# Expert weights from one-hot matrices: one multiplication for three parts, and second-key one-hots kept in DRAM

## The chip, the cores and the metric

The kernel runs on one core of a Trainium2 chip. The metric is the device time of one execution in microseconds (us). Engines are named as in the profile: PE multiplies matrices, PEld is its weight load, DVE, ACT and POOL are the vector, scalar and GpSimd engines, SP is the engine whose queue issues the loads of weights.

## The reference

One layer of a decoder trunk on 256 tokens with model width 2048. The first half (a convolution, a dilated attention, two gates) is not touched. The second half retrieves experts:

```python
s = jnp.einsum('bshpe,hpne->bshpn', qp, sub_keys)       # 8 heads, 2 keys of 128
v1, i1 = lax.top_k(s[..., 0, :], 16)
v2, i2 = lax.top_k(s[..., 1, :], 16)
cand = (v1[..., :, None] + v2[..., None, :]).reshape(B, S, 8, 256)
top, ci = lax.top_k(cand, 16)
e1 = jnp.take_along_axis(i1, ci // 16, axis=-1)
e2 = jnp.take_along_axis(i2, ci % 16, axis=-1)
idx = e1 * 128 + e2                                      # 8 x 16 experts of a token
g = jax.nn.softmax(top, axis=-1)
...
u = jnp.take(w_up, ic, axis=0)
a = jax.nn.gelu(jnp.einsum('td,tkd->tk', xc, u))
return jnp.einsum('tk,tkd->td', gc * a, jnp.take(w_down, ic, axis=0))
```

Everything is float32, and there are 128 x 128 = 16384 experts.

## The kernel before

The kernel does not gather. It computes the activation of every expert for every token (`up_unit`), multiplies it by a gate that is zero for the experts that a token did not choose, and multiplies the result by all of `w_down` (`down_unit`). Experts are counted by the first key e1 (128 rows of 128 experts), and rows go in four quarters q of EQ = 32. Two buffers, `CB[0]` and `CB[1]`, hold one quarter each.

A float32 weight is split in two float32r parts: ACT copies it into `hi` (`split_a`, L84), and DVE or POOL subtracts to give `lo` (`split_b`, L88). A product is then three matmuls: hi by hi, hi by lo, lo by hi. Of an up half (1024 of a row's 2048 columns) DVE first transposes the 32 x 32 blocks (`wt`, L1250).

The gate is made by `gate_c(p)`. For p = 0 it serves quarters 0 and 1, for p = 1 quarters 2 and 3. It works on blocks of NT = 8 tokens, 32 blocks in all. The partitions are the 128 (head, choice) pairs of a token. `build(b)` makes on DVE three things in bfloat16: `oh2`, the one-hots of the second key (128 values x 8 tokens); `oh1`, the one-hots of the first key (64 values x 8 tokens, those of the two quarters); and `ohg`, oh1 times each of three bfloat16 parts of the gate weight, which together give its float32 value (`gp`, made in `topk`). Tokens are interleaved in pairs, so that the innermost dimension has two tokens. `product(b)` is 24 matmuls on PE (L1347), 8 tokens by 3 parts, with oh2 of a token as weights (128 columns) and ohg as the moving operand (64 columns), into `gps` in PSUM. `apply(b)` multiplies one half of gps into `CB[0]` on DVE (L1354) and copies the other half into `CB[1]` on ACT (L1359). A step of the generator emits apply(b-2), build(b) and product(b-1) in this order.

The stream `st` puts everything in order by hand. For each half s it emits the ACT copy of half s+3, the subtraction of half s+2, then what is due (the step of the gate), then the matmuls of half s. In the two stretches of this document one step of the gate goes with each half:

- The first stretch (p = 0) runs beside up units of quarter 1, whose `lo` is all made by POOL (`busy`).
- The second stretch (p = 1) runs beside the down units of quarter 1 with d = 1, whose `lo` is all made by DVE. Eight of its 32 rows (`whole and n == 1`) are not split: PE multiplies them in float32 (`mm_whole`, L1458), straight from the loaded weight and from `CB`, and neither ACT nor DVE touches them.

For a split row, ACT also copies the row of C into `cch` (L1413) and DVE subtracts it into `ccl` (L1418). Buffers: four raw tiles of 1 MB, four of `hi`, three of `lo`, two of `wt`, `oh2` and `ohg`, one of `oh1`. In the profile oh1 and oh2 are both named `oh`: L1331 makes oh2, L1334 oh1, L1338 ohg. The tile `CB[..]` is named `C`.

Of the kernel before, what the change touches and what calls it, by code (L numbers as in the profile page):

```python
# [10 lines left out]
BF = mybir.dt.bfloat16  # L11
# [3 lines left out]
OP = mybir.AluOpType  # L15
# [3 lines left out]
P = 128  # L19
T = 256  # L20
# [13 lines left out]
EQ = 32  # L34
# [32 lines left out]
def layer_kernel(ctx, tc, x, c, norm1_g, norm2_g, w_ada, b_ada, w_in, conv_dw, conv_db, conv_ln_g,  # L67
                 conv_ln_b, w_conv_out, b_conv_out, q_norm_g, k_norm_g, w_attn_o, w_out, peer_w_q,
                 peer_sub_keys, peer_w_up, peer_w_down, out):
    nc = tc.nc  # L70
# [6 lines left out]
    main = ctx.enter_context(tc.tile_pool(name="main", bufs=1))  # L77
    dram = ctx.enter_context(tc.tile_pool(name="dram", bufs=1, space=bass.MemoryType.DRAM))
    x1_dram = dram.tile([P, 2, D], F32, name="x1_dram")


    def split_a(h, src):
# [157 lines left out]
    T2 = {}  # L240
# [818 lines left out]
    def open_p2():  # L1059
        pool = p2.enter_context(tc.tile_pool(name="p2", bufs=1))  # L1060
        T2["pool"] = pool
        CB[:] = [pool.tile([P, EQ * T], F32, name=f"C{i}") for i in range(2)]
        T2["keys"], T2["keysT"] = CB[0][:, 0:2048], CB[0][:, 2048:4096]
        nc.gpsimd.dma_start(T2["keys"].rearrange("p (a e) -> p a e", a=16),
                            dap(peer_sub_keys, 0, [[P, P], [P * P, 16], [1, P]]))
        T2["scr"] = CB[1]
        it = pool.tile([P, P, 2], BF, name="iota_rep")
        nc.gpsimd.iota(it, pattern=[[1, P], [0, 2]], base=0, channel_multiplier=0, allow_small_or_imprecise_dtypes=True)
        T2["iota"] = it
        T2["e1T"] = pool.tile([P, T], BF, name="e1T")  # L1070
        T2["e2T"] = pool.tile([P, T], BF, name="e2T")
        T2["gp"] = pool.tile([P, 3, T], BF, name="gp")

    def keys_t():
        for a0 in range(0, 16, 4):
# [81 lines left out]
    def topk():  # L1157
# [14 lines left out]
        for t in range(2):  # L1172
            vals, idx = tk["vals", t], tk["idx", t]
            nc.vector.tensor_copy(idb, idx)
            cand = scr[:, 4096:6144]
            v4 = vals.rearrange("p (h q) a -> p h q a", q=2)
            c4 = cand.rearrange("p (h a b) -> p h a b", h=H8, a=TOPK)
            for hs in halves:
                nc.vector.tensor_tensor(c4[:, hs], v4[:, hs, 0, :, None].to_broadcast([P, H8 // 2, TOPK, TOPK]),
                                        v4[:, hs, 1, None, :].to_broadcast([P, H8 // 2, TOPK, TOPK]), op=OP.add)  # L1180
                yield 1.2, 0
            for h in range(0, H8, 2):
                yield from top16([(top[:, b], ci[:, b], cand[:, b * 256:(b + 1) * 256]) for b in (h, h + 1)], 0.42)

            nc.vector.tensor_copy(den[:, 0], top[:, :, 0])
            nc.vector.tensor_tensor(top, top, den[:, 0, :, None].to_broadcast([P, H8, TOPK]), op=OP.subtract)
            nc.scalar.activation(top, top, AF.Exp)

            nc.vector.tensor_scalar(ca, ci, 4, None, op0=OP.logical_shift_right)
            nc.vector.tensor_copy(cab[:, 0], ca)  # L1190
            nc.vector.tensor_scalar(ca, ci, 15, None, op0=OP.bitwise_and)
            nc.vector.tensor_copy(cab[:, 1], ca)
            nc.vector.tensor_reduce(den[:, 1], top, axis=AX, op=OP.add)
            nc.vector.reciprocal(den[:, 1], den[:, 1])
            nc.vector.tensor_tensor(top, top, den[:, 1, :, None].to_broadcast([P, H8, TOPK]), op=OP.mult)
            yield 1.5, 0
            eq = scr[:, 6144:7168].bitcast(BF).rearrange("p (h a k) -> p h a k", h=H8, a=TOPK)
            pr = scr[:, 7168:8192].bitcast(BF).rearrange("p (h a k) -> p h a k", h=H8, a=TOPK)
            i4 = idb.rearrange("p (h q) a -> p h q a", q=2)
            shape = [P, H8 // 2, TOPK, TOPK]  # L1200
            for q in range(2):
                for hs in halves:
                    nc.vector.tensor_tensor(eq[:, hs], cab[:, q, hs, None, :].to_broadcast(shape),
                                            iota16[:, None].to_broadcast(shape), op=OP.is_equal)
                    yield 0.7, 0
                    nc.vector.tensor_tensor(pr[:, hs], eq[:, hs], i4[:, hs, q, :, None].to_broadcast(shape), op=OP.mult)
                    yield 1.2, 0
                    nc.vector.tensor_reduce(ee[:, q, hs], pr[:, hs].rearrange("p h a k -> p h k a"), axis=AX, op=OP.add)
                    yield 1.2, 0
            ts = slice(t * P, (t + 1) * P)  # L1210
            pt = T2["ps"].tile([P, 3, P], F32, name="eT", tag="m", bufs=2)
            yield 0.0, 4
            for q in range(2):
                nc.tensor.transpose(pt[:, q, :], ee[:, q].rearrange("p h k -> p (h k)"), ident)
            nc.tensor.transpose(pt[:, 2, :], top.rearrange("p h k -> p (h k)"), ident)
            nc.scalar.copy(T2["e1T"][:, ts], pt[:, 0, :])
            nc.scalar.copy(T2["e2T"][:, ts], pt[:, 1, :])

            gp = T2["gp"]
            nc.scalar.copy(gp[:, 0, ts], pt[:, 2, :])  # L1220
            nc.vector.tensor_tensor(rest, pt[:, 2, :], gp[:, 0, ts], op=OP.subtract)
            nc.vector.tensor_copy(gp[:, 1, ts], rest)
            nc.vector.tensor_tensor(rest, rest, gp[:, 1, ts], op=OP.subtract)
            nc.vector.tensor_copy(gp[:, 2, ts], rest)
            yield 1.0, 0

    topk_gen = topk()
# [49 lines left out]
    NT = 8  # L1277
    late = []

    def c_row(q, r, n=1):  # L1280
        if q < 3:
            return CB[q % 2][:, r * T:(r + n) * T]
        return CB[1].rearrange("p (b e t) -> p e b t", e=EQ, t=NT)[:, r:r + n]
# [37 lines left out]
    def gate_c(p):  # L1321
        nb = T // NT
        state = {}

        def build(b):

            pairs = lambda v: v.rearrange("p (b t) -> p b t", t=2)
            ts = slice(b * NT, (b + 1) * NT)
            nb2, ne = NT // 2, 2 * EQ
            o2 = T2["pool"].tile([P, nb2, P, 2], BF, name="oh2", tag="oh2", bufs=2)  # L1330
            nc.vector.tensor_tensor(o2, T2["iota"][:, None].to_broadcast([P, nb2, P, 2]),  # L1331
                                    pairs(T2["e2T"][:, ts])[:, :, None].to_broadcast([P, nb2, P, 2]), op=OP.is_equal)
            o1 = T2["pool"].tile([P, nb2, ne, 2], BF, name="oh1", tag="oh1", bufs=1)
            nc.vector.tensor_tensor(o1, T2["iota"][:, None, p * ne:(p + 1) * ne].to_broadcast([P, nb2, ne, 2]),  # L1334
                                    pairs(T2["e1T"][:, ts])[:, :, None].to_broadcast([P, nb2, ne, 2]), op=OP.is_equal)
            og = T2["pool"].tile([P, 3, nb2, ne, 2], BF, name="ohg", tag="ohg", bufs=2)
            for i in range(3):
                nc.vector.tensor_tensor(og[:, i], o1, pairs(T2["gp"][:, i, ts])[:, :, None].to_broadcast([P, nb2, ne, 2]),  # L1338
                                        op=OP.mult)
            state["o", b] = o2, og  # L1340

        def product(b):
            o2, og = state.pop(("o", b))
            ps = T2["ps"].tile([P, NT, 2 * EQ], F32, name="gps", tag="m", bufs=2)
            for t in range(NT):
                for i in range(3):
                    nc.tensor.matmul(ps[:, t, :], lhsT=o2[:, t // 2, :, t % 2], rhs=og[:, i, t // 2, :, t % 2],  # L1347
                                     start=i == 0, stop=i == 2)
            state["p", b] = ps.rearrange("p t e -> p e t")

# [10 lines left out]
        for b in range(nb + 2):  # L1361
            if 0 <= b - 2 < nb:
                apply(b - 2)
            if b < nb:
                build(b)
            if 0 <= b - 1 < nb:
                product(b - 1)
            yield

    gates = [gate_c(p) for p in range(2)]  # L1370
# [13 lines left out]
            return v, c_row(q, rr)  # L1384
        return v.rearrange("p (b t) -> p b t", t=NT), c_row(q, rr)[:, 0]

    def down_unit(q, d, r, whole=False):


        u = Unit(None, [])  # L1390
        e1 = q * EQ + r
# [7 lines left out]
        for n in range(2):  # L1399
# [52 lines left out]
                    for c in range(2):  # L1452
                        products(h, t, c, (1,), False, last)

            def mm_whole(h, rr=rr, n=n):
                for t in range(2):
                    for c in range(2):
                        nc.tensor.matmul(Y["ps"][t][c], lhsT=c_row(q, rr)[:, t * P:(t + 1) * P],  # L1458
                                         rhs=u.raw[:, n * 1024 + c * 512:n * 1024 + (c + 1) * 512], start=False, stop=rr == EQ - 1)

            h.a, h.b, h.mm = a, b, mm
            h.early_b = d == 1
            if whole and n == 1:
                h.a, h.b, h.mm, h.rel = None, None, mm_whole, "m"
            if rr == EQ - 1 and not (q == 3 and d == 1):
                h.after = [lambda: [y_done(q, d, Y["ps"], t, c) for t in range(2) for c in range(2)]]
            u.halves.append(h)
# [61 lines left out]
    for q in range(4):  # L1529
# [8 lines left out]
            add_units([downs[i] if kind else ups[i]], 0.25)  # L1538
        assert q < 1 or not ada_list
        m1 = len(st.halves)  # L1540
        downs = [down_unit(q, 1, r, q == 1 and r % 4 == 2) for r in range(0, EQ, 2)]
        if q == 1:
            for u in downs:
                for h in u.halves:
# [71 lines left out]
```

## Time and profile before

| what | value |
|---|---|
| median of 3 runs | 2517.66 us (2516.47 to 2523.12) |
| profiled execution: its own time | 2518.21 us |
| its span, first to last instruction | 2516.4 us |
| PE busy | 2426.6 us (96%) |
| DVE busy | 1854.2 us (74%) |
| ACT busy | 1120.8 us (45%) |
| POOL busy | 530.3 us (21%) |
| DMA | 518.73 MB, mean 206 GB/s |

The profile counts an instruction as busy from its start to its end, also while it waits for something inside. Spans on POOL are rough. The first stretch lies between 1162.8 and 1310 us of the span, the second between 1849 and 1972 us.

### The profile page before, as it was taken

To read this page: it belongs to the slowest core of one execution; us is meant where nothing else is said; L and a number is where in the kernel's file an instruction comes from. 1 tells how busy PE (TensorE), PEld (TensorE's weight loads), DVE (VectorE), ACT (ScalarE), POOL (GpSimd) and SP (SyncE) were. 2 spreads that over 40 slices of the span, in tenths; PEclk is the share of its full clock that TensorE was granted. 3 is DMA by queue.
4 is the path that set the end of the run, shared out by engine and by line. 5 is a ranking of instruction groups with operands and counts; after the bars stand their busy time and mean duration, and the time that the engine had idled before them with its cause. 6 is when DMAs were issued, how large, how long until landed. Compare 5 with 4: busy or idle time off the path is not lost.

```text
span 2516.4 us, 39750 instructions
## 1 busy us (share of the span) xinstructions
PE 2426.6 (96%) x15728; PEld 2056.6 (82%) x15728; DVE 1854.2 (74%) x2642; ACT 1120.8 (45%) x1477; POOL 530.3 (21%) x262
## 2 busy tenths in 40 slices
PE   7999889999999899988999999999999999999998
PEld 4667677777766799988889988999987899988877
DVE  2655679886454569897998787877799777667776
ACT  5333345444334444443335555555443344445454
POOL 1000000000000007786552234332000111124023
PEclk9999999999999999999999999999999999999999
DMA  9887346777899978777557866899844777766563
GB/s 329 297 301 251 117 136 210 257 251 267 279 298 294 204 159 178 158 167 152 110 124 220 234 218 194 222 226 238 204 156 135 185 181 185 188 186 214 194 209 117
DMA packets 261178, 518.73 MB, mean 206 GB/s; under 512 B 16400, under 2 KB 57568, under 8 KB 260352
## 3 DMA queue, kind: packets, MB, share of 16 engines
q1 hardware_dynamic: 258912, 507.61, 70.4%
q0 software_dynamic: 2048, 8.58, 1.0%
q8 instruction: 123, 2.02, 0.4%
q14 instruction: 63, 0.52, 0.1%
q10 hardware_dynamic: 32, 0.01, 0.0%
HBM read 511.94 MB, written 4.19 MB: 205 GB/s over the span
## 4 chain that ended last, share of the span: by engine, by line
PE 71%; DVE 10%; POOL 3%; issue 2%; DMA 1%; ACT 1%; SPq 0%; DVEq 0%; POOLq 0%; ACTq 0%
PE aps L1267 6%; PE aps L1265 6%; PE aps L1266 6%; PE y L1435 6%; PE y L1436 6%; PE y L1438 5%; PE z L429 5%; PE z L431 4%; PE z L430 4%; PE z L1436 3%; PE z L1438 3%; PE z L1435 3%; POOL lo L88 3%; DVE wt L1250 2%; PE ada L330 2%
## 5 line engine op out<-in xcount | busy, mean ns | idle before, releaser
L88 DVE TENSOR_TENSOR lo<-raw,hi 128x1024 fp32r<-128x1024 f32 x456 | 561.8, 1237 | 376.3 <-issue 112.6
L84 ACT CAST hi<-raw 128x1024 fp32r<-128x1024 f32 x504 | 526.6, 1051 | 520.6 <-PE zv L559 103.1
L1267 PE MATMUL aps<-h2hi,lo 128*128 128x256 f32 x2048 | 582.0, 284 | 8.6 <-POOL lo L88 8.5
L1265 PE MATMUL aps<-h2hi,hi 128*128 128x256 f32 x2048 | 584.3, 285 | 0.4 <-ACT hi L84 0.4
L1266 PE MATMUL aps<-h2lo,hi 128*128 128x256 f32 x2048 | 580.7, 284 | 0.0
L84 ACT CAST hi<-wt 128x1024 fp32r<-128x1024 f32 x256 | 269.3, 1052 | 470.7 <-DVE wt L1250 427.6
L88 POOL TENSOR_TENSOR lo<-wt,hi 128x1024 fp32r<-128x1024 f32 x116 | 292.7, 2529 | 611.1 <-PE aps L1267 497.1
L1267 PEld LDWEIGHTS aps<-h2hi,lo 128*128 128x128 f32 x2048 | 394.0, 192 | 11.2 <-POOL lo L88 11.2
L1265 PEld LDWEIGHTS aps<-h2hi,hi 128*128 128x128 f32 x2048 | 394.1, 192 | 2.6 <-ACT hi L84 0.6
L1266 PEld LDWEIGHTS aps<-h2lo,hi 128*128 128x128 f32 x2048 | 394.3, 193 | 2.0 <-issue 0.2
L1250 DVE STREAM_TRANSPOSE wt<-raw 128x1024 f32<-128x1024 f32 x256 | 315.8, 1237 | 28.2 <-POOL lo L88 23.7
L1418 DVE TENSOR_TENSOR ccl<-C,cch 128x256 fp32r<-128x256 f32 x248 | 198.9, 803 | 96.7 <-PE z L1438 57.6
L1435 PE MATMUL y<-hi,cch 128*128 128x512 f32 x608 | 241.1, 397 | 0.0
L1436 PE MATMUL y<-lo,cch 128*128 128x512 f32 x608 | 237.3, 390 | 0.0
L88 DVE TENSOR_TENSOR lo<-wt,hi 128x1024 fp32r<-128x1024 f32 x140 | 171.8, 1229 | 27.3 <-PE aps L1267 14.0
L1438 PE MATMUL y<-hi,ccl 128*128 128x512 f32 x608 | 187.6, 390 | 0.0
L88 POOL TENSOR_TENSOR lo<-raw,hi 128x1024 fp32r<-128x1024 f32 x48 | 117.0, 2436 | 245.9 <-PE z L1436 123.6
L347 POOL TENSOR_TENSOR acc<-acc,raw 128x512 f32<-128x512 f32 x60 | 101.4, 1689 | 261.0 <-ACT raw L346 240.3
L1413 ACT CAST cch<-C 128x256 fp32r<-128x256 f32 x248 | 99.8, 403 | 123.6 <-PE z L1436 101.9
L1436 PE MATMUL z<-lo,cch 128*128 128x512 f32 x384 | 149.5, 389 | 2.2 <-DVE lo L88 2.2
L1435 PE MATMUL z<-hi,cch 128*128 128x512 f32 x384 | 149.5, 389 | 1.0 <-ACT cch L1413 1.0
L1438 PEld LDWEIGHTS y<-hi,ccl 128*128 128x128 f32 x608 | 114.2, 188 | 24.4
(295 smaller groups left out, 3965.7 us busy)
## 6 DMA issues: line engine op xcount, KB each, us to landing
raw<-in_peer_w_up_dram SPq DMA_DIRECT2D x512, 256.0 KB, 6.0
raw<-in_peer_w_down_dram SPq DMA_DIRECT2D x128, 1024.0 KB, 5.1
raw<-in_w_ada_dram SPq DMA_DIRECT2D x86, 1024.0 KB, 7.1
raw<-in_w_in_dram SPq DMA_DIRECT2D x73, 1024.0 KB, 5.3
raw<-in_w_out_dram SPq DMA_DIRECT2D x64, 256.0 KB, 5.2
raw<-in_peer_w_q_dram SPq DMA_DIRECT2D x64, 256.0 KB, 7.1
raw<-in_w_in_dram SPq DMA_DIRECT2D x22, 512.0 KB, 8.9
raw<-in_w_ada_dram SPq DMA_DIRECT2D x20, 512.0 KB, 5.2
```

The costliest lines, as they stand in the source:

```text
L84: nc.scalar.copy(h.hi, src)
L88: eng.tensor_tensor(h.lo, src, h.hi.bitcast(F32), op=OP.subtract)
L347: nc.gpsimd.tensor_tensor(acc, acc, src, op=OP.add)
L429: nc.tensor.matmul(z, lhsT=ah, rhs=hi[:, kk], start=first, stop=False)
L1250: nc.vector.transpose(wt.rearrange("p j g a -> p g j a"), u.raw.rearrange("p (g j a) -> p g j a", g=4, a=32)[:, :, n * 8:(n + 1) * 8, :])
L1265: nc.tensor.matmul(z, lhsT=hi[:, jj], rhs=qh["hi"][:, j, :], start=j == 0, stop=False)
L1266: nc.tensor.matmul(z, lhsT=hi[:, jj], rhs=qh["lo"][:, j, :], start=False, stop=False)
L1267: nc.tensor.matmul(z, lhsT=lo[:, jj], rhs=qh["hi"][:, j, :], start=False, stop=j == NK - 1)
L1418: nc.vector.tensor_tensor(cl, row, ch, op=OP.subtract)
L1435: nc.tensor.matmul(z, lhsT=ch, rhs=hi, start=first, stop=False)
L1436: nc.tensor.matmul(z, lhsT=ch, rhs=lo, start=False, stop=False)
L1438: nc.tensor.matmul(z, lhsT=cl, rhs=hi, start=False, stop=last)
```

## The change

The three multiplications of oh1 by the parts of the weight become one, with the three parts side by side in `ohg` and in `gp`. The moving operand of a matmul of `product` then steps by 6 elements (12 bytes) in place of 2 (4 bytes). In the first stretch each oh2 is also written to DRAM (256 KB, issued from ACT's queue); in the second stretch it is not computed but read back (256 KB per block, issued from ACT's queue one step ahead, behind product(b-1)). The second stretch has no float32 rows any more: `mm_whole` is gone, and all 32 rows are split.

```diff
+    o2_dram = [dram.tile([P, 1024], BF, name=f"o2_dram{b}") for b in range(T // 8)]
...
-        T2["gp"] = pool.tile([P, 3, T], BF, name="gp")
+        T2["gp"] = pool.tile([P, T // 2, 3, 2], BF, name="gp")
...
-            gp = T2["gp"]
-            nc.scalar.copy(gp[:, 0, ts], pt[:, 2, :])
-            nc.vector.tensor_tensor(rest, pt[:, 2, :], gp[:, 0, ts], op=OP.subtract)
...
+            gp = T2["gp"][:, t * P // 2:(t + 1) * P // 2]
+            pair = lambda v: v.rearrange("p (b t) -> p b t", t=2)
+            nc.scalar.copy(gp[:, :, 0], pair(pt[:, 2, :]))
+            nc.vector.tensor_tensor(pair(rest), pair(pt[:, 2, :]), gp[:, :, 0], op=OP.subtract)
...
+        def fetch(b):
+            o2 = T2["pool"].tile([P, NT // 2, P, 2], BF, name="oh2", tag="oh2", bufs=2)
+            state["o2", b] = o2
+            if p == 1:
+
+                nc.scalar.dma_start(o2.rearrange("p b e t -> p (b e t)"), o2_dram[b])
+
         def build(b):
...
-            o2 = T2["pool"].tile([P, nb2, P, 2], BF, name="oh2", tag="oh2", bufs=2)
-            nc.vector.tensor_tensor(o2, T2["iota"][:, None].to_broadcast([P, nb2, P, 2]),
-                                    pairs(T2["e2T"][:, ts])[:, :, None].to_broadcast([P, nb2, P, 2]), op=OP.is_equal)
+            if p == 0:
+                fetch(b)
+            o2 = state.pop(("o2", b))
+            if p == 0:
+                nc.vector.tensor_tensor(o2, T2["iota"][:, None].to_broadcast([P, nb2, P, 2]),
+                                        pairs(T2["e2T"][:, ts])[:, :, None].to_broadcast([P, nb2, P, 2]), op=OP.is_equal)
+                nc.scalar.dma_start(o2_dram[b], o2.rearrange("p b e t -> p (b e t)"))
...
-            og = T2["pool"].tile([P, 3, nb2, ne, 2], BF, name="ohg", tag="ohg", bufs=2)
-            for i in range(3):
-                nc.vector.tensor_tensor(og[:, i], o1, pairs(T2["gp"][:, i, ts])[:, :, None].to_broadcast([P, nb2, ne, 2]),
-                                        op=OP.mult)
+
+            og = T2["pool"].tile([P, nb2, ne, 3, 2], BF, name="ohg", tag="ohg", bufs=2)
+            shape = [P, nb2, ne, 3, 2]
+            nc.vector.tensor_tensor(og, o1[:, :, :, None].to_broadcast(shape),
+                                    T2["gp"][:, b * nb2:(b + 1) * nb2, None].to_broadcast(shape), op=OP.mult)
...
-                    nc.tensor.matmul(ps[:, t, :], lhsT=o2[:, t // 2, :, t % 2], rhs=og[:, i, t // 2, :, t % 2],
+                    nc.tensor.matmul(ps[:, t, :], lhsT=o2[:, t // 2, :, t % 2], rhs=og[:, t // 2, :, i, t % 2],
...
+            if p == 1 and b == 0:
+                fetch(0)
             if b < nb:
                 build(b)
             if 0 <= b - 1 < nb:
                 product(b - 1)
+            if p == 1 and b + 1 < nb:
+                fetch(b + 1)
...
-            if whole and n == 1:
-                h.a, h.b, h.mm, h.rel = None, None, mm_whole, "m"
...
-        downs = [down_unit(q, 1, r, q == 1 and r % 4 == 2) for r in range(0, EQ, 2)]
+        downs = [down_unit(q, 1, r) for r in range(0, EQ, 2)]
```

## Rows read from the trace of the kernel before

**Rows 1.** Busy time of each engine in three windows, the first stretch in two.

```profile
core 0: us, PE busy (x) PEld busy (x) DVE busy (x) ACT busy (x) POOL busy (x), PEclk, DMA share, GB/s
1173.80:1213.70 39.90, 31.86 (x382) 30.47 (x381) 39.69 (x49) 11.53 (x18) 20.04 (x8) 0.96 0.47 101
1213.70:1308.00 94.30, 88.48 (x1061) 83.38 (x1060) 93.52 (x155) 31.95 (x50) 56.55 (x22) 1.00 0.52 120
1850.00:1968.00 118.00, 117.48 (x1117) 86.53 (x1117) 114.22 (x241) 44.22 (x78) 0.00 (x0) 1.00 0.48 143
```

**Rows 2.** Timeline of DVE, first stretch: start and length in us.

```profile
1173.79 3.30 DVE L1338 TENSOR_TENSOR ohg<-oh,gp 128x512 bf16<-128x512 bf16 x3
...
1202.30 3.24 DVE L1338 TENSOR_TENSOR ohg<-oh,gp 128x512 bf16<-128x512 bf16 x3
...
1213.73 1.09 DVE L1338 TENSOR_TENSOR ohg<-oh,gp 128x512 bf16<-128x512 bf16 x3
...
1222.30 1.10 DVE L1338 TENSOR_TENSOR ohg<-oh,gp 128x512 bf16<-128x512 bf16 x3
1223.31 1.24 DVE L1250 STREAM_TRANSPOSE wt<-raw 128x1024 f32<-128x1024 f32 x1
1224.47 0.39 DVE L1354 TENSOR_TENSOR C<-gps,C 128x256 f32<-128x256 f32 x1
1224.78 1.42 DVE L1331 TENSOR_TENSOR oh<-iota_rep,e2T 128x1024 bf16<-128x1024 bf16 x1
1226.13 0.41 DVE L1334 TENSOR_TENSOR oh<-iota_rep,e1T 128x512 bf16<-128x512 bf16 x1
...
1307.95 1.10 DVE L1338 TENSOR_TENSOR ohg<-oh,gp 128x512 bf16<-128x512 bf16 x3
```

**Rows 3.** Timeline of POOL, first stretch, with idle time before and its releaser.

```profile
1202.66 2.60 POOL L88 TENSOR_TENSOR lo<-wt,hi 128x1024 fp32r<-128x1024 f32 x1 [1.28 <-PE aps L1267]
...
1223.09 2.57 POOL L88 TENSOR_TENSOR lo<-wt,hi 128x1024 fp32r<-128x1024 f32 x1 [1.70 <-PE aps L1267]
```

**Rows 4.** Timeline of PE, first stretch: one product and the next matmul.

```profile
1218.50 1.49 PE L1347 MATMUL gps<-ohg,oh 128*128 128x64 bf16 x24
...
1219.83 0.36 PE L1265 MATMUL aps<-h2hi,hi 128*128 128x256 f32 x1
```

**Rows 5.** Groups by form, 1770 to 1985 us: busy us, mean ns.

```profile
L88 DVE TENSOR_TENSOR lo<-raw,hi 128x1024 fp32r<-128x1024 f32 x34 | 41.5, 1222 | 13.9 <-issue 7.5 <-PE aps L1267 6.4
...
L1338 DVE TENSOR_TENSOR ohg<-oh,gp 128x512 bf16<-128x512 bf16 x96 | 35.1, 421 | 1.1
...
L1331 DVE TENSOR_TENSOR oh<-iota_rep,e2T 128x1024 bf16<-128x1024 bf16 x32 | 21.8, 681 | 0.0
```

**Rows 6.** Chain of waits, second stretch: start, length, what.

```profile
1877.73 3.51 PE y L1458 x8
...
1884.81 0.74 PE gps L1347 x24
...
1885.86 0.23 PE y L1436
...
1888.38 0.74 PE gps L1347 x24
```

**Rows 7.** Timeline of DVE, second stretch: two neighbouring steps.

```profile
1885.06 1.22 DVE L88 TENSOR_TENSOR lo<-raw,hi 128x1024 fp32r<-128x1024 f32 x1
...
1888.93 1.22 DVE L88 TENSOR_TENSOR lo<-raw,hi 128x1024 fp32r<-128x1024 f32 x1
```

**Rows 8.** Timeline of ACT: an issue at the start, then the second stretch.

```profile
0.74 0.42 ACTq L258 DMA_DIRECT2D stage<-in_c_dram  x1
...
1890.91 0.37 ACT L1359 COPY C<-gps 128x256 f32<-128x256 f32 x1 [1.44 <-DVE C L1354]
```

**Rows 9.** DMA issues by line: KB each, median us from issue to landing.

```profile
raw<-in_peer_w_down_dram SPq DMA_DIRECT2D x128, 1024.0 KB, 5.1
...
out_dram<-fin SPq DMA_DIRECT2D x8, 256.0 KB, 2.4
```

More of the change, by code (lines that the diff above doesn't have):

```diff
@@ L1217, in topk @@
             nc.scalar.copy(T2["e2T"][:, ts], pt[:, 1, :])
-            gp = T2["gp"]
-            nc.scalar.copy(gp[:, 0, ts], pt[:, 2, :])
-            nc.vector.tensor_tensor(rest, pt[:, 2, :], gp[:, 0, ts], op=OP.subtract)
-            nc.vector.tensor_copy(gp[:, 1, ts], rest)
-            nc.vector.tensor_tensor(rest, rest, gp[:, 1, ts], op=OP.subtract)
-            nc.vector.tensor_copy(gp[:, 2, ts], rest)
+            gp = T2["gp"][:, t * P // 2:(t + 1) * P // 2]
+            pair = lambda v: v.rearrange("p (b t) -> p b t", t=2)
+            nc.scalar.copy(gp[:, :, 0], pair(pt[:, 2, :]))
+            nc.vector.tensor_tensor(pair(rest), pair(pt[:, 2, :]), gp[:, :, 0], op=OP.subtract)
+            nc.vector.tensor_copy(gp[:, :, 1], pair(rest))
+            nc.vector.tensor_tensor(pair(rest), pair(rest), gp[:, :, 1], op=OP.subtract)
+            nc.vector.tensor_copy(gp[:, :, 2], pair(rest))
             yield 1.0, 0
@@ L1385, in row_views, with down_unit @@
         return v.rearrange("p (b t) -> p b t", t=NT), c_row(q, rr)[:, 0]
-    def down_unit(q, d, r, whole=False):
+    def down_unit(q, d, r):
         u = Unit(None, [])
@@ L1453, in mm @@
                         products(h, t, c, (1,), False, last)
[L1455 to L1459, printed above, removed]
             h.a, h.b, h.mm = a, b, mm
             h.early_b = d == 1
-            if whole and n == 1:
-                h.a, h.b, h.mm, h.rel = None, None, mm_whole, "m"
             if rr == EQ - 1 and not (q == 3 and d == 1):
```

## Prediction

> **What bounds the kernel now.** I read the busy times by window first, then the timelines of DVE and POOL side by side, then the chain of waits. They show two stretches with different limits, and the change lies in both and nowhere else.
>
> In the second stretch PE is the limit: it is busy 117.48 of 118.00 us at full clock [rows 1]. One step with a split row goes from one product to the next in 1888.38 - 1884.81 = 3.57 us; one with a float32 row is the product's 0.74 us and 3.51 us of L1458, 4.25 us [rows 6]. DVE needs 1888.93 - 1885.06 = 3.87 us for a split row [rows 7], slightly more than PE, and catches up in the float32 rows, where it has no lo and no ccl to make.
>
> In the first stretch DVE looks full (93.52 of 94.30 us), but some of that is waiting. Building oh2 takes 0.68 us where POOL is idle [rows 5] and 1.42 us here [rows 2]: it starts at 1224.78 and cannot work until POOL's subtraction, 1223.09 to 1225.66 [rows 3], is over. So the bfloat16 operations of DVE and the subtraction of POOL exclude each other, and the operation that comes second waits for the whole of the first. The step is POOL's 2.57 us, then oh2, oh1 and ohg, then POOL again: 22 steps from 1213.73 to 1307.95, 4.28 us each [rows 2]. The transpose and the multiplication from PSUM (1223.31 and 1224.47) run beside POOL. PE waits: a product of 0.74 us takes 1.49 us [rows 4, 6].
>
> Before 1213.7 it goes worse: 7 steps in 1213.73 - 1173.79 = 39.94 us, 5.71 us each [rows 2], and PE is busy only 31.86 of 39.90 us [rows 1]. The triple at 1202.30 takes 3.24 us in place of 1.10 because POOL's subtraction starts at 1202.66, after the first of the three multiplications, and the other two stand behind it [rows 2, 3]. DVE then does transpose and multiplication alone, with POOL idle, and the overlap of the good steps is lost.
>
> **The change part by part.** *One multiplication for three.* 512 elements take 421 ns, 1024 take 681 ns [rows 5]: 0.508 ns per element. If the new form keeps this rate, 1536 elements take 421 + 1024 x 0.508 = 941 ns. Three take 1.01 us from the first's start to the next operation (1222.30 to 1223.31), so neighbours overlap by (3 x 421 - 1010) / 3 = 84 ns and the new one occupies 0.86 us. It saves 0.15 us per block. The other bound is a rate like that of float32, 1222 ns for 1024 elements [rows 5]: 1.83 us, 1.75 after the overlap, 0.74 more than today. I take 0.86, as two neighbours remain the innermost dimension in every operand.
>
> [...]
>
> *The first stretch.* A good step falls by 0.15 to 4.13 us, as both sides of the exclusion (POOL, then the one-hots) lie in it. And between the three parts there is no gap any more into which POOL can slip: a request that comes during the multiplication waits until its end, and POOL then runs beside the transpose, which is the good order. So I count the seven bad steps as good ones, less one that is still disturbed (1.6 us, a bad step less a good one): 29 x 4.13 + 1.6 = 121.4 us in place of 39.94 + 94.22 = 134.2, 12.8 us less.
>
> *The writes to DRAM* (32 of 256 KB) stand in ACT's queue behind the building of oh2. Queued behind them are ACT's next `hi` copies, which wait for a transpose that DVE does after oh2 anyhow. An issue costs ACT 0.42 us [rows 8]; ACT is busy 31.95 of 94.30 us [rows 1]. The buffer is wanted again two steps later, 8.3 us less oh2's own 0.7; a 256 KB transfer lands in 2.4 us alone, and 1 MB in 5.1 us under load [rows 9]. Nothing is added; without this cover a late landing would stop DVE. Traffic rises from 120 GB/s by 256 KB per 4.13 us, 63 GB/s, at a DMA share of 0.52 [rows 1].
>
> *The second stretch.* oh2 leaves DVE (0.60 us of its pitch: 0.68 less the overlap), the multiplication gives back 0.15: 3.87 - 0.75 = 3.12 us for a split row, below PE's 3.57. So PE can go through 32 split rows, and eight steps of 4.25 become 3.57: 8 x 0.68 = 5.4 us less. ACT gets eight `hi` and `cch` copies and 32 issues more; it is busy 44.22 of 118 us. The rewriting of `gp` in topk (two blocks of small copies) I cost at nothing: it runs beside matmuls of up units; uncovered it would be under 1 us.
>
> *The fetches.* One stands in ACT's queue behind the copy out of gps, which waits for DVE's multiplication (the 1.44 us in [rows 8]). Within a step, with PE's previous matmuls as zero, DVE does lo, ccl and C (1.22 + 0.34 + 0.42, about 2.0), ACT copies until 2.3 and issues. Behind it only the next step's copies are queued, which need PE's matmuls of this step. The block is wanted two steps after zero, at 7.1: 4.8 us for the landing, against 2.4 alone and 5.1 for four times the bytes [rows 9]. I take it as hidden, except for the first block, which is fetched only one step ahead: 1.5 us.
>
> *The moving operand of the product* steps by 12 bytes. Today 24 matmuls of 64 columns take 0.74 us, 31 ns each, with a step of 4 bytes [rows 6]. Below, no cost; above, the nearest row of a slower stream is float32, 3.51 / 8 = 0.44 us for 512 columns against 0.23 in float32r [rows 6], 1.9 times: 0.67 us more per product. I take nothing, the row that has the same two-byte data; both ends stay in the range.
>
> [...] No trace here has a step above 4 bytes.
>
> **Sum.** -12.8 in the first stretch, -5.4 + 1.5 in the second: -16.7 on the profiled execution's 2518.21 us, 2501.5. Its time is 0.55 above the median of the runs, so 2501 us. What a measurement can tell from no change is about 0.3%, 7.6 us: below 2510.1 is faster, above 2525.2 slower.
>
> **Rivals.**
> 1. *POOL still slips in*, between oh1 and the multiplication say, and the bad steps stay. For it: these gaps remain, and three operations still stand in a row. Against: in 22 of 29 steps the order, once found, held even with three gaps more. Then 29 x 0.15 = 4.4 less in the first stretch, 3.9 in the second: 2509.
> 2. *The 12-byte step slows the product.* PE has some 0.75 us to spare in a good step of the first stretch [rows 4], which becomes 0.60, and none in the second. At half the upper bound (0.34) the second stretch loses 31 x 0.34 = 10.5: 2511.5. At the bound (0.67) it loses 20.8, the first 29 x 0.07 = 2: 2524. From 0.13 us per product on, the second stretch is no faster than now (0.13 x 31 = 3.9).
> 3. *The multiplication falls to the float32 rate: slower.* For it: the operand that is repeated threefold has a new inner pattern that no row shows. Against: the weights are already repeated 64 times at full rate. A step of the first stretch becomes 4.28 + 0.74 = 5.02, 147.2 us in place of 134.2, 13.0 more; DVE in the second needs 3.87 - 0.60 + 0.74 = 4.01, 124.3 us for 31 steps against 23 x 3.57 + 8 x 4.25 = 116.1 now, 8.2 more, with 1.5 for the first fetch: 2540. It decides from 0.45 us above 3.12 on, where DVE passes PE.
> 4. *Fetches land late.* A block lands x us after the issue, and the next fetch into its buffer waits for the product: two steps take 2.3 + 0.42 + x. At 5.1 that is 3.91 per step, 31 x 0.34 = 10.5 more: 2511.5.
>
> **How the numbers follow.** My forecast has 0.50 (2496 to 2506: from an empty first-stretch margin to the multiplication with no gain of its own); bad steps stay 0.12; product slower by about half the bound 0.13, by all of it 0.08; float32 rate 0.07; late fetches 0.10. The range 2495 to 2519 leaves out the last 0.15 and a little below. Faster: 0.48 of the forecast, 0.08 of the bad steps, 0.05 of late fetches, 0.61. Slower: float32 rate 0.07 and 0.05 of the slow product, 0.12. The same: the rest, 0.27.
>
> **What would show it.** In the first stretch steps of 4.1 us from the start, multiplications near 0.94 us unless POOL holds them, and POOL's starts just behind them. In the second, steps of 3.57 us with PE busy throughout, products of 0.74 us, no L1458, and PE never waiting for a DMA. Wrong it is if products take 1 us or more, if the multiplication takes over 1.2 us with POOL idle, or if PE or ACT waits for the fetched blocks.

## The result, and the profile after

The changed kernel takes 2574.7 us (median of 4 runs, 2573.24 to 2575.15) against 2518.64 us (4 runs): 1.0216 times as long, interval 1.0203 to 1.0228. The forecast was 2501 us, faster. It was wrong in sign, by one term: the price of the 12-byte step. A second, smaller miss, in the fetches, shows only once the step is put right.

The chain of waits of the changed kernel, one line of the first stretch and three of the second, shows it (start, length, what):

```profile
1240.73 2.16 PE gps L1361 x24
...
1933.21 2.14 PE gps L1361 x24
1935.34 0.26 PE y L1452
...
1938.12 2.14 PE gps L1361 x24
```

A product takes 2.14 us where it took 0.74 [rows 6]; products of 1 us or more were the first sign of being wrong that the prediction named. (These are lengths in the chain, which counts from the end of the matmul before. The timeline counts from the product's own first matmul, which starts before that end, so that the same products have 2.29 and 0.90 us there.) A step of the second stretch is 1938.12 - 1933.21 = 4.91 us, PE's own time throughout. The busy times by window say that PE is now the limit in both stretches:

```profile
core 0: us, PE busy (x) PEld busy (x) DVE busy (x) ACT busy (x) POOL busy (x), PEclk, DMA share, GB/s
1200.00:1300.00 100.00, 100.00 (x955) 99.14 (x954) 99.31 (x100) 28.82 (x45) 47.88 (x20) 1.00 0.64 157
1900.00:2000.00 100.00, 100.00 (x735) 86.18 (x733) 65.36 (x104) 36.73 (x61) 0.00 (x0) 1.00 0.51 156
```

In the first stretch it was DVE and POOL excluding each other [rows 1 to 3]: oh2 took 1.42 us there, 0.68 where POOL was idle [rows 2, 5]. From the first to the last product the second stretch takes 152.3 us (1869.16 to 2021.49) in place of 116.0 (1850.56 to 1966.60), 36.3 more, and it begins 18.6 us later: together 54.9 of the 57.0 us by which the span grew.

What the prediction said of DVE holds. Its timeline, first in the first stretch and then in the second:

```profile
1297.01 2.33 DVE L1343 TENSOR_TENSOR oh<-iota_rep,e2T 128x1024 bf16<-128x1024 bf16 x1
1299.26 0.41 DVE L1347 TENSOR_TENSOR oh<-iota_rep,e1T 128x512 bf16<-128x512 bf16 x1
1299.70 0.96 DVE L1352 TENSOR_TENSOR ohg<-oh,gp 128x1536 bf16<-128x1536 bf16 x1
...
1304.75 0.96 DVE L1352 TENSOR_TENSOR ohg<-oh,gp 128x1536 bf16<-128x1536 bf16 x1
...
1905.64 0.96 DVE L1352 TENSOR_TENSOR ohg<-oh,gp 128x1536 bf16<-128x1536 bf16 x1
1908.28 1.23 DVE L89 TENSOR_TENSOR lo<-raw,hi 128x1024 fp32r<-128x1024 f32 x1 [1.68 <-PE y L1453]
```

The one multiplication takes 0.96 us. In the second stretch DVE waits some 1.7 us in every step for PE to free a buffer of `lo`. In the first, steps are 5.05 us from the second on. The 2.33 us of oh2 still hold the wait for POOL, which now costs nothing: PE is busy 100.00 of 100.00 us.

### The profile page after: what moved, and what is told of

Read it like the earlier page. It is cut to its first block, busy times and chain, and to the rows that moved or that the text cites. A ratio compares the mean times of both kernels' runs of the same rounds, so it can differ in the third digit from the quotient of the medians.

```text
span 2573.4 us, 39854 instructions
## 1 busy us (share of the span) xinstructions
PE 2501.8 (97%) x15760; PEld 2146.4 (83%) x15760; DVE 1856.2 (72%) x2498; ACT 1134.4 (44%) x1493; POOL 526.6 (20%) x262
## 4 chain that ended last, share of the span: by engine, by line
PE 79%; DVE 4%; POOL 3%; issue 2%; ACT 1%; DMA 0%; SPq 0%; DVEq 0%; POOLq 0%; ACTq 0%
PE aps L1267 8%; PE aps L1269 8%; PE aps L1268 8%; PE y L1452 6%; PE y L1453 6%; PE y L1455 6%; PE gps L1361 5%; PE z L430 5%; PE z L432 5%; PE z L431 5%; PE z L1453 3%; PE z L1452 3%; PE z L1455 3%; POOL lo L89 3%; PE ada L331 2%
## 5 line engine op out<-in xcount | busy, mean ns | idle before, releaser
L89 DVE TENSOR_TENSOR lo<-raw,hi 128x1024 fp32r<-128x1024 f32 x464 | 572.0, 1237 | 420.4 <-issue 108.0
L85 ACT CAST hi<-raw 128x1024 fp32r<-128x1024 f32 x512 | 535.1, 1051 | 520.5 <-PE zv L560 105.1
L1452 PE MATMUL y<-hi,cch 128*128 128x512 f32 x640 | 254.4, 397 | 0.0
L1453 PE MATMUL y<-lo,cch 128*128 128x512 f32 x640 | 249.8, 390 | 0.0
L1455 PE MATMUL y<-hi,ccl 128*128 128x512 f32 x640 | 197.5, 390 | 0.0
L1361 PE MATMUL gps<-ohg,oh 128*128 128x64 bf16 x1536 | 147.5, 269 | 4.8 <-DVE ohg L1352 4.8
```

The costliest lines, as they stand in the source:

```text
L85: nc.scalar.copy(h.hi, src)
L89: eng.tensor_tensor(h.lo, src, h.hi.bitcast(F32), op=OP.subtract)
L1452: nc.tensor.matmul(z, lhsT=ch, rhs=hi, start=first, stop=False)
L1453: nc.tensor.matmul(z, lhsT=ch, rhs=lo, start=False, stop=False)
L1455: nc.tensor.matmul(z, lhsT=cl, rhs=hi, start=False, stop=last)
```

## The experiments

Theory 1: the 12-byte step of the moving operand is the whole loss. Theory 2: the traffic of oh2 or the one multiplication causes it, and PE only shows it. The kernel before was measured again beside the runs: 2520.09 us beside the first four, 2519.82 us beside the next two. Differences and ratios are against these.

**The layout alone taken back.** The one multiplication stays, and the parts lie outside the first-key values.

```diff
-            og = T2["pool"].tile([P, nb2, ne, 3, 2], BF, name="ohg", tag="ohg", bufs=2)
-            shape = [P, nb2, ne, 3, 2]
-            nc.vector.tensor_tensor(og, o1[:, :, :, None].to_broadcast(shape),
-                                    T2["gp"][:, b * nb2:(b + 1) * nb2, None].to_broadcast(shape), op=OP.mult)
+            og = T2["pool"].tile([P, nb2, 3, ne, 2], BF, name="ohg", tag="ohg", bufs=2)
+            shape = [P, nb2, 3, ne, 2]
+            nc.vector.tensor_tensor(og, o1[:, :, None].to_broadcast(shape),
+                                    T2["gp"][:, b * nb2:(b + 1) * nb2, :, None].to_broadcast(shape), op=OP.mult)
...
-                    nc.tensor.matmul(ps[:, t, :], lhsT=o2[:, t // 2, :, t % 2], rhs=og[:, t // 2, :, i, t % 2],
+                    nc.tensor.matmul(ps[:, t, :], lhsT=o2[:, t // 2, :, t % 2], rhs=og[:, t // 2, i, :, t % 2],
```

> The changed kernel with the three parts outside the first-key values: ohg is [4 pairs, 3 parts, 64 values, 2 tokens], made by one multiplication as in the changed kernel, and the moving operand of the product steps by 4 bytes again; the copies of oh2 in DRAM and the 32 split rows stay. Theory 1 (the 12-byte step of the moving operand is the whole loss): products fall from 2.14 us to 0.74, the rest of the prediction comes true, 2501 us (2495 to 2510), 0.993 of before. Theory 2 (the loss is in the traffic of oh2 or in the one multiplication, and PE only shows it): products stay above 1.5 us and the time above 2540 us.

Measured: 2509.49 us, 0.9956 of before (0.9942 to 0.9969). Theory 2 falls: the same bytes go to and from DRAM, and 65 us are gone. But of the forecast gain of 16.7 us only 10.6 came; 6 are missing. The timeline of PE in the second stretch shows where (products only; in brackets the idle time before and what ended it):

```profile
1928.67 0.90 PE L1361 MATMUL gps<-ohg,oh 128*128 128x64 bf16 x24
1933.99 0.90 PE L1361 MATMUL gps<-ohg,oh 128*128 128x64 bf16 x24 [1.59 <-DMA oh<-o_dram]
1937.57 0.90 PE L1361 MATMUL gps<-ohg,oh 128*128 128x64 bf16 x24
...
1966.90 0.90 PE L1361 MATMUL gps<-ohg,oh 128*128 128x64 bf16 x24 [1.88 <-DMA oh<-o_dram]
```

The first 22 steps are 3.57 us each, as forecast. From 1928.67 to the last product at 1966.90, nine steps take 38.23 us in place of 32.1: four products wait for a fetched block. A fetch is issued 5.3 us before its product could start (1926.90 for the one at 1932.24). The fetches before that landed in 2.4 to 5.1 us, in time; the four late ones took 6.8 to 7.0. The first of these in the view of DMA issues, and SP's first loads of the next up units in its timeline:

```profile
oh<-o_dram ACTq DMA_DIRECT2D x1, 256.0 KB, 7.0
...
1933.31 16.83 SPq L1243 DMA_DIRECT2D raw<-in_peer_w_up_dram  x8
```

Three of the four were issued after 1933.31, beside those loads. The first was already 6.4 us under way then, 0.7 us behind the issue of a 1 MB load (1926.16); so the loads of the up units are not the whole reason, and what lengthens a landing stays open. (The span of this profiled execution, 2517.5 us, lies above the timed median; it had lost 4.5 us before the first stretch and 3.8 in that stretch's last step, so only single steps are read from it.)

**The one multiplication alone**, in that layout, on the kernel before: no copies in DRAM, eight float32 rows.

```diff
-        T2["gp"] = pool.tile([P, 3, T], BF, name="gp")
+        T2["gp"] = pool.tile([P, T // 2, 3, 2], BF, name="gp")
...
-            for i in range(3):
-                nc.vector.tensor_tensor(og[:, i], o1, pairs(T2["gp"][:, i, ts])[:, :, None].to_broadcast([P, nb2, ne, 2]),
-                                        op=OP.mult)
+            shape = [P, nb2, 3, ne, 2]
+            nc.vector.tensor_tensor(og, o1[:, :, None].to_broadcast(shape),
+                                    T2["gp"][:, b * nb2:(b + 1) * nb2, :, None].to_broadcast(shape), op=OP.mult)
...
-                    nc.tensor.matmul(ps[:, t, :], lhsT=o2[:, t // 2, :, t % 2], rhs=og[:, i, t // 2, :, t % 2],
+                    nc.tensor.matmul(ps[:, t, :], lhsT=o2[:, t // 2, :, t % 2], rhs=og[:, t // 2, i, :, t % 2],
```

> The kernel before with only the one multiplication, in the layout of the 4-byte step: oh2 is computed in both stretches, the eight float32 rows stay, no copies in DRAM. Theory 1: the first stretch has steps of 4.13 us from the start, 12.8 us less, and the second is bound by PE as before, 2505 us. Rival inside theory 1 (POOL still slips in between oh1 and the multiplication, the bad steps stay): 4.4 us less, 2514 us. Theory 2 (the one multiplication is at fault): above 2540 us.

Measured: 2507.64 us, 0.9951 (0.9937 to 0.9965), that is 12.4 us less against 12.8 forecast. The timeline of DVE, first stretch:

```profile
1173.11 0.96 DVE L1340 TENSOR_TENSOR ohg<-oh,gp 128x1536 bf16<-128x1536 bf16 x1
...
1233.01 1.44 DVE L1332 TENSOR_TENSOR oh<-iota_rep,e2T 128x1024 bf16<-128x1024 bf16 x1
1234.37 0.41 DVE L1335 TENSOR_TENSOR oh<-iota_rep,e1T 128x512 bf16<-128x512 bf16 x1
1234.82 0.96 DVE L1340 TENSOR_TENSOR ohg<-oh,gp 128x1536 bf16<-128x1536 bf16 x1
1235.70 1.24 DVE L1251 STREAM_TRANSPOSE wt<-raw 128x1024 f32<-128x1024 f32 x1
...
1238.99 0.96 DVE L1340 TENSOR_TENSOR ohg<-oh,gp 128x1536 bf16<-128x1536 bf16 x1
...
1297.34 0.96 DVE L1340 TENSOR_TENSOR ohg<-oh,gp 128x1536 bf16<-128x1536 bf16 x1
```

Steps are 1238.99 - 1234.82 = 4.17 us (4.13 forecast), and all of them from the fourth on are so: the seven bad steps of before [rows 2] do not come. The rival in which POOL still slips in falls. From the third multiplication to the last, the 29 steps that the prediction counts, it is 1297.34 - 1173.11 = 124.2 us, where 121.4 was forecast and 134.2 was before: 9.9 us less. One disturbed step at the start took 7.55 us (to 1180.66) where 5.7 was counted. The other 2.5 of the 12.4 us do not lie in this stretch, so that the time meets the forecast this closely is partly luck.

**The copies in DRAM and the split rows alone**, with three multiplications and a 4-byte step.

```diff
-            og = T2["pool"].tile([P, nb2, ne, 3, 2], BF, name="ohg", tag="ohg", bufs=2)
...
+            og = T2["pool"].tile([P, 3, nb2, ne, 2], BF, name="ohg", tag="ohg", bufs=2)
+            for i in range(3):
+                nc.vector.tensor_tensor(og[:, i], o1, T2["gp"][:, b * nb2:(b + 1) * nb2, i][:, :, None].to_broadcast([P, nb2, ne, 2]),
+                                        op=OP.mult)
...
-                    nc.tensor.matmul(ps[:, t, :], lhsT=o2[:, t // 2, :, t % 2], rhs=og[:, t // 2, :, i, t % 2],
+                    nc.tensor.matmul(ps[:, t, :], lhsT=o2[:, t // 2, :, t % 2], rhs=og[:, i, t // 2, :, t % 2],
```

> The changed kernel with three multiplications and a 4-byte step as before: only the copies of oh2 in DRAM and the 32 split rows are left of the change. Theory 1: eight rows by 0.68 us less and 1.5 us for the first fetch, 3.9 us less in the second stretch, nothing in the first, 2514 us. Theory 2 (the traffic is at fault): above 2540 us.

Measured: 2520.25 us, 1.0003 (0.9994 to 1.0012). Neither theory: no loss, but no gain. After a first step of 3.95 us the second stretch has 23 steps of 3.57 us, and then seven that together take 4.8 us more than that, four products waiting for their block; 5.4 us were to be won. Two of the four in the timeline of PE:

```profile
1942.85 0.90 PE L1361 MATMUL gps<-ohg,oh 128*128 128x64 bf16 x24 [1.06 <-DMA oh<-o_dram]
...
1967.86 0.90 PE L1361 MATMUL gps<-ohg,oh 128*128 128x64 bf16 x24 [1.82 <-DMA oh<-o_dram]
```

The first stretch keeps the disturbed steps of before, so that their going in the run above comes from the one multiplication.

**The step alone**, on the kernel before: three multiplications write the parts side by side.

```diff
-            og = T2["pool"].tile([P, 3, nb2, ne, 2], BF, name="ohg", tag="ohg", bufs=2)
+            og = T2["pool"].tile([P, nb2, ne, 3, 2], BF, name="ohg", tag="ohg", bufs=2)
             for i in range(3):
-                nc.vector.tensor_tensor(og[:, i], o1, pairs(T2["gp"][:, i, ts])[:, :, None].to_broadcast([P, nb2, ne, 2]),
+                nc.vector.tensor_tensor(og[:, :, :, i], o1, pairs(T2["gp"][:, i, ts])[:, :, None].to_broadcast([P, nb2, ne, 2]),
                                         op=OP.mult)
...
-                    nc.tensor.matmul(ps[:, t, :], lhsT=o2[:, t // 2, :, t % 2], rhs=og[:, i, t // 2, :, t % 2],
+                    nc.tensor.matmul(ps[:, t, :], lhsT=o2[:, t // 2, :, t % 2], rhs=og[:, t // 2, :, i, t % 2],
```

> The kernel before with only the layout of ohg changed: the three multiplications write the parts side by side, so that the moving operand steps by 12 bytes; nothing else. Theory 1: a product takes 2.15 us; the first stretch has steps of 5.05 us (31 of them, 157 us in place of 141), the second 4.97 us for a split and 5.65 us for a float32 row (159.5 us in place of 116): 59 us more, about 2577 us. Theory 2: within 5 us of the kernel before.

Measured: 2579.58 us, 1.0234 (1.0219 to 1.0250), 59 us more. Products and one float32 row in the timeline of PE, second stretch:

```profile
1905.34 2.29 PE L1347 MATMUL gps<-ohg,oh 128*128 128x64 bf16 x24
...
1907.45 3.64 PE L1458 MATMUL y<-raw,C 128*128 128x512 f32 x8
...
1910.93 2.29 PE L1347 MATMUL gps<-ohg,oh 128*128 128x64 bf16 x24
...
1915.84 2.29 PE L1347 MATMUL gps<-ohg,oh 128*128 128x64 bf16 x24
```

A float32 row takes 5.59 us, a split one 4.91. The step alone accounts for the loss. The rest of the change gave the changed kernel some of it back: its second stretch takes 152.3 us, this one's 157.6, which is the price of the eight float32 rows. (The edit also makes DVE write at a step of 12 bytes; its price is in the last section. DVE does not set the pace here: between 1870 and 2020 us it waits 36.7 us for the products.)

**Fetches one more step ahead**, on the kernel with the layout taken back. The two buffers of `acc` are free in the second stretch.

```diff
+            tag = "acc" if p == 1 and b % 2 else "oh2"
-            o2 = T2["pool"].tile([P, NT // 2, P, 2], BF, name="oh2", tag="oh2", bufs=2)
+            o2 = T2["pool"].tile([P, NT // 2, P, 2], BF, name="oh2", tag=tag, bufs=2)
...
             if p == 1 and b == 0:
-                fetch(0)
+                for k in range(3):
+                    fetch(k)
...
-            if p == 1 and b + 1 < nb:
-                fetch(b + 1)
+            if p == 1 and 1 <= b and b + 2 < nb:
+                fetch(b + 2)
```

> The changed kernel with the 4-byte step and one multiplication, and the fetches one more step ahead: odd blocks of oh2 go into the two buffers of acc, which are free in the second stretch, so there are four buffers, three blocks are fetched at the start and block b+2 behind product(b-1). Theory (the fetches land late once the loads of the next up units run beside them, and this took back the gain of the second stretch): all 31 steps 3.57 us, no wait of PE for a DMA, about 6 us less than without it, 2503 us. Rival (the shared DMA engines hold up the loads of weights themselves, and the waits only move there): no gain, 2509 us.

Measured: 2502.88 us, 0.9934 (0.9920 to 0.9947), the fastest version here. Products in the timeline of PE, and the time to landing of the fetches of the second stretch from the view of the tile:

```profile
1925.47 0.90 PE L1362 MATMUL gps<-ohg,oh 128*128 128x64 bf16 x24
1929.04 0.90 PE L1362 MATMUL gps<-ohg,oh 128*128 128x64 bf16 x24
...
1943.34 0.90 PE L1362 MATMUL gps<-ohg,oh 128*128 128x64 bf16 x24
1947.64 0.88 PE L1362 MATMUL gps<-ohg,oh 128*128 128x64 bf16 x24 [0.57 <-DVE ohg L1353]
1952.64 0.89 PE L1362 MATMUL gps<-ohg,oh 128*128 128x64 bf16 x24 [1.28 <-DMA oh<-o_dram]
```

```profile
DMA to landing us min/median/max: 2.5/4.9/11.0
```

Landings are no earlier, up to 11.0 us, but PE waits for only one of them: the first 29 steps are 3.57 us each, also where they were delayed before. Before the last two products, after steps of 4.30 and 5.00 us, PE waits 0.57 us for DVE and then 1.28 us for the last block, the one that took 11.0 us (issued at 1941.55). So the expectation of no wait at all misses by that one. The rival, that loads of weights are held up in their place and nothing is gained, falls: the 6 us came.

**No float32 rows without copies in DRAM**, on the kernel with the one multiplication alone.

```diff
-        downs = [down_unit(q, 1, r, q == 1 and r % 4 == 2) for r in range(0, EQ, 2)]
+        downs = [down_unit(q, 1, r) for r in range(0, EQ, 2)]
```

> The kernel before with the one multiplication in the 4-byte layout and without float32 rows, but without any copy of oh2 in DRAM: DVE computes oh2 in the second stretch too. Theory (DVE then needs 3.87 less 0.15, 3.72 us for a step, and sets the pace): 31 steps of 3.72 us, 115.3 us against 115.4 in the kernel with the eight float32 rows: within 2 us of 2507 us. Rival (DVE's lag is carried by buffers and PE's 3.57 us rule): 110.7 us, 2502 us.

Measured: 2511.55 us, 0.9965 (0.9953 to 0.9977). In the timeline of DVE, second stretch:

```profile
1890.88 1.22 DVE L88 TENSOR_TENSOR lo<-raw,hi 128x1024 fp32r<-128x1024 f32 x1
...
1893.73 0.96 DVE L1340 TENSOR_TENSOR ohg<-oh,gp 128x1536 bf16<-128x1536 bf16 x1
1894.61 1.22 DVE L88 TENSOR_TENSOR lo<-raw,hi 128x1024 fp32r<-128x1024 f32 x1
```

DVE's step is 3.73 us (3.72 expected) and sets the pace, so the rival falls; the stretch takes 117.6 us against 115.4 with the float32 rows. The time is 4 us above that kernel's, taken beside other runs of the kernel before, where at most 2 were expected. The stretch holds 2.2 of them (its last two steps, 4.86 and 4.52 us, wait for DVE); 1.7 lie ahead of the first product of the first stretch, where the two kernels are the same. Taking the float32 rows out gains nothing while oh2 is still made on DVE.

**The disputed cost by itself.** Nothing of the layer is computed but series of equal matmuls; x is written out with some of their results.

```python
def view(tile_, n, s):
    return tile_[:, 0:n * s].rearrange("p (e s) -> p e s", s=s)[:, :, 0]
...
for s in STEPS:                       # 2 to 32 bytes
    run(f"n64step{s}b", 64, w4, view(mov, 64, s // 2))   # 240 matmuls
```

> Leaves the whole layer out: it only runs series of 240 equal matmuls and writes x with some of their results. The step of the moving operand goes from 2 to 32 bytes in bfloat16 with 64 and 256 columns and from 4 to 32 bytes in float32r with 256; in one series it is the weights that step by 2 to 12 bytes. [...] Steps of the weights change nothing while the load hides behind the matmul.

Groups by line (busy us, mean ns of one; busy / 240 is the time from one to the next):

```profile
L48 PE MATMUL r256step16b<-movr,wtr 128*128 128x256 f32 x240 | 56.2, 413 | 0.0
...
L48 PE MATMUL r256step8b<-movr,wtr 128*128 128x256 f32 x240 | 54.6, 407 | 0.0
L48 PE MATMUL r256step32b<-movr,wtr 128*128 128x256 f32 x240 | 52.4, 397 | 0.0
L48 PE MATMUL r256step4b<-movr,wtr 128*128 128x256 f32 x240 | 29.0, 283 | 0.0
...
L48 PE MATMUL n64step32b<-mov,wts 128*128 128x64 bf16 x240 | 28.7, 299 | 0.0
L48 PE MATMUL n64step16b<-mov,wts 128*128 128x64 bf16 x240 | 28.2, 297 | 0.0
...
L48 PE MATMUL n64step12b<-mov,wts 128*128 128x64 bf16 x240 | 21.8, 271 | 0.0
...
L48 PE MATMUL n64step8b<-mov,wts 128*128 128x64 bf16 x240 | 14.9, 241 | 0.0
...
L48 PE MATMUL weights12b<-mov,wts 128*128 128x64 bf16 x240 | 11.4, 212 | 0.0
L48 PE MATMUL n64step6b<-mov,wts 128*128 128x64 bf16 x240 | 11.4, 211 | 0.0
...
L48 PE MATMUL n64step4b<-mov,wts 128*128 128x64 bf16 x240 | 7.4, 193 | 0.0
L48 PE MATMUL n64step2b<-mov,wts 128*128 128x64 bf16 x240 | 7.2, 193 | 0.0
```

A matmul of 64 bfloat16 columns takes 30 ns with a step of 2 bytes, 31 with 4, 47 with 6, 62 with 8, 91 with 12, 118 with 16 and 120 with 32. The 12 bytes come out near the 89 ns of the changed kernel (2.14 us for 24), so the price is there without the rest of that kernel. At 6 and 8 bytes the time has already risen: of the steps tried, none above 4 bytes was free. It goes with the step up to 16 bytes, and 32 bytes take 2 ns more than 16. A step of 12 bytes in the weights costs time too, 47 ns against the 31 with both steps at 4 bytes, where no change was expected. Why a longer step takes longer is not shown. The numbers have two limits. From 12 bytes on the 64-column series ran at a granted clock of 0.50 (last section); only for 12 bytes does the changed kernel give a time at full clock. And they do not carry over to float32r, where a column at a step of 16 bytes takes 234 / 256 = 0.91 ns, against 118 / 64 = 1.84 here.

## Why the prediction was wrong

*The step that failed: "The moving operand of the product".* I took nothing, by "the row that has the same two-byte data", and made the upper end from float32, 1.9 times and 0.67 us. Measured is 2.9 times and 1.40 us per product. No row had a bfloat16 operand with a longer step, and the float32 matmul of L1458 reads its columns at a step of 4 bytes, so its 1.9 times are the price of a data type and no bound on a step. The rival had the right mechanism and place; at 0.08 for the full price and 2524 us for its end it was undersized. With 1.40 us in its formula, the second stretch is 31 x (3.57 + 1.40) = 154 us; measured 152.3. In the first, a step of 5.05 us against 4.17 with the step put right leaves 0.88 of the 1.40: PE's spare time covered 0.52. (The prediction had 0.60, from 1.49 us of the timeline less 0.74 of the chain, two views that do not count alike.)

No trace of the kernel before had a price for a step above 4 bytes; the nothing in the sum was the author's estimate. The series shows one at full clock: 47 ns at 6 bytes and 62 at 8 in place of 31.

*The one multiplication: right.* 0.958 us against 0.941 forecast, alike in the changed kernel and in both layouts tried. No run shows it without a gain of its own, the case at the 2506 us of the forecast: it occupies 1235.70 - 1234.82 = 0.88 us where the three took 1.01. The float32-rate rival falls.

*The first stretch: right in the mechanism and nearly in the size*, once PE is not the limit: 4.17 us for 4.13 and the bad steps gone but for one, 9.9 us less in the stretch for 12.8 forecast.

*The writes: hidden* in every step of the changed kernel; with the 4-byte step late writes were seen to stop DVE, for 2.4 us before 1302.9 in the kernel with the layout taken back and for 0.8 us in the fastest version.

*The second stretch: right in PE's 3.57 us for each of 22 steps*, and DVE's slack.

*The fetches: wrong at the end of the stretch.* I allowed 4.8 us for a landing and took it as hidden. The median landing was 4.7 us, at that edge, and four of 6.8 to 7.0 us took the gain back. Fetching further ahead returned it. A row of the kernel before that [rows 9] leaves out was nearer than both of its rows, the same size under load:

```profile
raw<-in_peer_w_up_dram SPq DMA_DIRECT2D x512, 256.0 KB, 6.0
```

 The loss on the first block, 1.5 us, was not seen (3.56 us in its step with the layout taken back). In the changed kernel PE's own slowness hid the fetches but for 0.3 us. (Its view of waits also puts 28.7 us of idle time before ACT's copies into `cch` down to fetched blocks, a sign that the prediction had named; PE was busy throughout, so it cost nothing.)

The sum for everything but the step, -16.7 us, is met by the version with both repairs: 2502.88 against 2519.82 us, -16.9. That it is met to 0.2 us is luck: the interval of that run goes from -13 to -20 us, and the two profiled spans differ by 14.7.

## What to carry to other kernels

The layout that suits one engine is read by the next: when an operation is widened, look at the step with which the matmul reads its result, and put the small dimension outside (here 2.14 us for a product at 12 bytes, 0.74 at 4). A cost that no row of the trace shows deserves a bound of its own or a short series of measurements, not the ratio of a neighbouring data type. A transfer whose allowance equals its median landing is not hidden (here 4.8 us allowed, a median of 4.7, and four of 6.8 to 7.0); count it with the longest landing, and look for a row of the same size under load.

## What the runs showed of the hardware

In float32r with 256 columns the steps above 4 bytes cost about the same, 228 ns at 8 bytes, 234 at 16 and 218 at 32, against 121 at 4, all at a granted clock of 1.00: no rise with the step as in bfloat16. Why the two types differ stays open.

The granted clock fell from 1.00 to 0.50 within the series, with PE busy without a break in the profile. Windows of the series of 64 columns, steps of 4, 8 and 12 bytes (the columns are those of the windows above, without ACT):

```profile
37.30:44.50 7.20, 7.20 (x244) 7.20 (x241) 0.17 (x1) 0.00 (x0) 1.00 0.02 5
...
55.80:70.40 14.60, 14.60 (x242) 14.60 (x240) 0.17 (x1) 0.00 (x0) 1.00 0.01 2
...
88.10:109.60 21.50, 21.50 (x243) 21.50 (x241) 0.17 (x1) 0.00 (x0) 0.50 0.01 2
```

It was 1.00 up to the 8-byte series and 0.50 from the 12-byte one to that of 32 bytes, with the 10-byte series of 74 ns each between them (0.59). Twelve bytes take 91 ns at 0.50 and 2.14 / 24 = 89 ns in the changed kernel at 1.00: they differ by 2 ns, so the lower clock of the series does not explain the price of this step. In the changed kernel, with products between other matmuls, the clock was 1.00 in both windows.

The DVE multiplications that write pairs at a step of 12 bytes (the run with the step alone) take 491 ns for 512 elements (median) in place of 419, a smaller price than PE's for reading them.
